# Hidden columns of a SwiGLU feed-forward in tiles of 126 instead of 128

## The chip, the cores and the metric

One core of a Trainium2 chip runs the whole kernel. The metric is the device time of one execution in microseconds, the median over several runs. All arithmetic is in float32; TensorE does it through pairs of rounded parts, as told below.

## The reference

One layer of a flow-matching backbone over 512 latent tokens and 256 context tokens, 2048 features each: a modulated RMSNorm, one input projection shared by gated linear attention and a gated short convolution, one output projection with a gated residual, then a second modulated RMSNorm and a SwiGLU feed-forward with a hidden width of 5632, a gated residual and a last RMSNorm. The part that the change touches:

```python
def swiglu(h, wg, wu, wd):
    return (jax.nn.silu(h @ wg) * (h @ wu)) @ wd

h2 = modulate(rmsnorm(x_next, norm2_g[i]), sh2, sc2)
x_next = x_next + gt2 * swiglu(h2, w_ffn_gate[i], w_ffn_up[i], w_ffn_down[i])
...
return rmsnorm(x, final_g)
```

## The kernel before

Activations lie transposed: features on the 128 partitions, the 512 tokens along the row. Every product is written as three matmuls (`mm3`, L78): both operands are kept as a high part (rounded by a cast on ScalarE) and a low part (the difference, by VectorE), and low x high, high x low and high x high are added up in PSUM. A unit of weights is 128 x 1024 numbers, 512 KB. `load_w` (L106) brings one unit into one of four `raw` buffers by a DMA that SP issues (L103), casts it to `whi` (L87) and subtracts to `wlo` (L88); there are three buffers of each. All matmuls stand at L75.

The feed-forward part begins at L761. The hidden width of 5632 is cut into `HT` = 44 tiles of 128, and the tiles into groups of eight: five groups of eight and one of four. For each hidden tile, `proj_units` multiplies two units of gate weights and two of up weights with the 16 feature tiles of `h2` into the PSUM banks `ag` and `au`, 48 matmuls each. The trace calls a matmul by these names. `swiglu` (L762) makes silu(ag) x au and splits it into the pair `act`. When a group is done, its down pass runs over the 16 output tiles: it loads a unit of `wfd`, multiplies it with the group's `act` pairs into `acc` (24 matmuls for a group of eight) and adds the gated result to the residual `xn` (L793). The last group is done by halves of the tokens, so that the final norm of the first half lies beside the second half's matmuls.

In the first group VectorE also works off the last 16 tiles of the modulation: `mod_some` (L343) loads two half rows of `wm2` per tile through the same `raw` buffers and sums each against `cbc` (L351). It is called after each hidden tile but the first:

```python
            run(proj_units(ag, wfg[ht], h2), proj_units(au, wfu[ht], h2))
            swiglu(ag, au, act[-1], ALL)
            mod_some(2.5, 64)
        if gi == 0:
            mod_finish(48, 64)
```

With 2.5, two and three tiles alternate. The first hidden tile goes by halves of the tokens together with the norm. In this text the hidden tiles of the first group are numbered from 0, and a tile's four units are its two of gate and its two of up weights.

The order on each engine is made by a scheduler when the kernel is built: instructions of one engine may stand in another order than in the code, and each engine then goes through its own list strictly.

Of the kernel before, what the change touches and what calls it, by code (L numbers as in the profile page):

```python
# [28 lines left out]
HT = FFN // P  # L29
# [4 lines left out]
# columns of the "cols" input  # L34
C_G1, C_G2, C_FG, C_BMOD, C_GLA, C_CONV = 0, 16, 32, 48, 144, 146
NCOLS = 170
# square constant blocks of the "cst" input
B_ID, B_TRIF, B_TRIB, B_SUFF, B_SUFB, B_MF, B_MB, B_ONE, B_ONE16, B_SELX, B_SELC = range(11)
NBLK = 11
# columns of the "sm" input  # L40
# [5 lines left out]
def tile_hybrid_block(  # L46
# [30 lines left out]
    def mm3(o, l, r, start, stop):  # L77
        """l, r: (high, low) parts; the three products that float32 can hold."""  # L78
        mm(o, l[1], r[0], start, False)
        mm(o, l[0], r[1], False, False)  # L80
        mm(o, l[0], r[0], False, stop)
# [8 lines left out]
    def split_scaled(hi, lo, src, scale):  # L90
        """Parts of src * scale, with a scale per partition."""
        nc.scalar.activation(hi, src, AF.Copy, scale=scale)
        nc.vector.scalar_tensor_tensor(lo, src, scale, hi.bitcast(F32), op0=ALU.mult, op1=ALU.subtract)  # L93

    def split_shifted(hi, lo, src, shift):
        """Parts of src + shift, with a shift per partition."""
        nc.scalar.activation(hi, src, AF.Identity, bias=shift)
        nc.vector.scalar_tensor_tensor(lo, src, shift, hi.bitcast(F32), op0=ALU.add, op1=ALU.subtract)  # L98
# [7 lines left out]
    def load_w(src, k, eng=None):  # L106
        """One unit of weights, split into its parts, as [128, k, n]."""
        r = load_raw(src)
        n = r.shape[-1]
        hi = wpool.tile([P, 1024], F32R, tag="whi", name="whi", bufs=3)  # L110
        lo = wpool.tile([P, 1024], F32R, tag="wlo", name="wlo", bufs=3)
        split(hi[:, :n], lo[:, :n], r, eng)
        return (hi[:, :n].rearrange("p (k n) -> p k n", k=k),
                lo[:, :n].rearrange("p (k n) -> p k n", k=k))
# [7 lines left out]
    def rsqrt_of_sum(pool, s, scale, n):  # L122
        """1 / sqrt(s * scale + eps): square root and reciprocal, then one Newton step."""
        ms = pool.tile([P, n], F32, tag="rs_m", name="rs_m", bufs=2)
        t = pool.tile([P, n], F32, tag="rs_t", name="rs_t", bufs=2)
        r = pool.tile([P, n], F32, tag="rs_r", name="rs_r", bufs=2)
        nc.vector.tensor_scalar(ms, s, scale, EPS, op0=ALU.mult, op1=ALU.add)
        nc.scalar.activation(t, ms, AF.Sqrt)
        nc.vector.reciprocal(r, t)
        nc.vector.tensor_tensor(t, r, r, op=ALU.mult)  # L130
        nc.vector.tensor_tensor(t, t, ms, op=ALU.mult)
        nc.vector.tensor_scalar(t, t, -0.5, 1.5, op0=ALU.mult, op1=ALU.add)
        nc.vector.tensor_tensor(r, r, t, op=ALU.mult)
        return r

    def row_bcast(ps, pool, r):
        """ps[m, 128 * tt + t] = r[t, tt] for every m."""
        for tt in range(r.shape[-1]):
            dg = pool.tile([P, P], F32, tag="rb_d", name="rb_d", bufs=2)
            nc.vector.tensor_scalar(dg, ident, r[:, tt : tt + 1], None, op0=ALU.mult)  # L140
            mm(tok(ps, tt), ones, dg, tt == 0, True)

# [15 lines left out]
    # ======== K projection behind the stream of the scale columns ========  # L158
    # The rows of x and ctx are scaled by g1 * (1 + scale) only: their norm and the shift's share
    # are applied to the products of this part and the next.  # L160
# [12 lines left out]
    # Silu of the zeros brings in the table before c is there  # L173
# [3 lines left out]
    def mod_cols(src, c0, n):  # L177
        """silu(c) and silu(c_ctx) times n * 128 columns of w_mod: [128 columns, n, (x, ctx)] in PSUM."""
# [92 lines left out]
    # ======== V projection of heads 0 and 1 behind the stream of the shift columns ========  # L271
# [6 lines left out]
    def shift_chunk(i):  # L278
        """Chunk i of hx and hc from the scaled rows: norm, then the shift."""
        for n, h, rb, q in ((SEQ, hx[i], rbx, 0), (CTX, hc[i], rbc, 1)):  # L280
            t = hcpool.tile([P, n], F32, tag=f"sq{q}", name="ht", bufs=2)
            nc.gpsimd.tensor_tensor(t, h[0].bitcast(F32), h[1].bitcast(F32), op=ALU.add)
            nc.vector.tensor_tensor(t, t, rb, op=ALU.mult)
            sh = shs[:, i, q : q + 1]
            if q == 0:
                nc.vector.tensor_scalar(t, t, sh, None, op0=ALU.add)
                split(h[0], h[1], t)
                hraw[i] = t
            else:
                split_shifted(h[0], h[1], t, sh)  # L290
# [10 lines left out]
    def lf_finish(pl, a, n):  # L301
        """Sum of the four partial sums, as rows of lfT."""
# [41 lines left out]
    def mod_some(n, last):  # L344
        """n more of the tiles of 128 features; n may be a fraction."""
# [15 lines left out]
    # ======== V projection of heads 2 and 3; the shift's share of K and of the first V ========  # L361
    def shares(i):
        """Chunk i of the low rank of ctx, and one unit of weights of bias = shift @ w."""
# [65 lines left out]
    def log_gates(pool, tag, pzs, las):  # L429
        """la = log_sigmoid(z) = min(z, 0) - ln(1 + exp(-|z|)); its 1 / 16 is in the constants."""  # L430
# [8 lines left out]
    def proj_units(acc, wsrc, x, units=(0, 1), part=ALL):  # L439
        """acc = (weight columns)^T x, for one tile of 128 columns; yields after each unit of weights."""  # L440
        for n, u in enumerate(units):
            w = load_w(wsrc[u], 8)
            for k in range(8):
                mm3(acc[:, part], sl(w, ALL, k), sl(x[8 * u + k], ALL, part), n == 0 and k == 0, n == 1 and k == 7)
            yield

    def proj_pair(accs, wsrcs, x, units, part, ws=None, eng=None):
        """Two tiles of columns over one part of the tokens, side by side; ws: the first units, if at hand;
        eng: what makes the low parts of the first units, if not VectorE.

        Returns the last units."""
        for n, u in enumerate(units):
# [4 lines left out]
            for k, (acc, w) in ([(k, a) for a in aw for k in range(8)] if kept else  # L457
                                [(k, a) for k in range(8) for a in aw]):
                mm3(acc[:, part], sl(w, ALL, k), sl(x[8 * u + k], ALL, part), n == 0 and k == 0, n == 1 and k == 7)
# [7 lines left out]
    # ======== context states ========  # L467
# [54 lines left out]
    def weave(stages, fill):  # L522
        """A chain's stages between units of the projections, so that TensorE has work while it waits."""
# [9 lines left out]
    # ======== gated linear attention per head, gated short convolution in between ========  # L533
# [17 lines left out]
    def do_gla(h):  # L551
        """One head over blocks of 128 tokens; within a block, decays are relative to its middle."""
# [7 lines left out]
        for d in range(2):  # L560
# [8 lines left out]
            # the column of the middle, whose own decay is one, carries the decay from the block's start to it  # L569
# [26 lines left out]
        # o as [tokens, values], two blocks of tokens to a bank  # L596
# [25 lines left out]
        # per-head norm  # L622
# [8 lines left out]
        # back to [values, tokens]; gain and swish gate  # L631
# [43 lines left out]
    # ======== output projection, gated residual ========  # L675
# [17 lines left out]
    def square(m, t, acc):  # L693
        """Adds t^2 to acc."""
# [5 lines left out]
    def row_scale(sums):  # L700
        """1 / rms of the rows of one half, the same on every partition; sums: tiles of squares to add up."""
# [11 lines left out]
    # the last two tiles go by halves of the tokens, so that the norm of the first half is hidden  # L713
# [47 lines left out]
    # ======== FFN ========  # L761
    def swiglu(ag, au, dst, part):  # L762
        t = big()[:, part]
        nc.scalar.activation(t, ag[:, part], AF.Silu)  # L764
        nc.vector.tensor_tensor(t, t, au[:, part], op=ALU.mult)
        split(dst[0][:, part], dst[1][:, part], t)

    groups = [(8 * g, min(8, HT - 8 * g)) for g in range((HT + 7) // 8)]
    for gi, (h0, nh) in enumerate(groups):
        act = []  # L770
        for ht in range(h0, h0 + nh):
# [11 lines left out]
            mod_some(2.5, 64)  # L783
# [4 lines left out]
        for m in range(KD):  # L788
            acc = abank("acc")
            w = load_w(wfd[m][:, h0 * P : (h0 + nh) * P], nh)  # L790
            for k in range(nh):
                mm3(acc, sl(w, ALL, k), act[k], k == 0, k == nh - 1)
            nc.vector.scalar_tensor_tensor(xn[m], acc, modv[:, 48 + m : 49 + m], xn[m], op0=ALU.mult, op1=ALU.add)  # L793

    # ======== last part of the FFN and final norm, by halves of the tokens ========
    put_t = {}

    def put(i, hf, rb):
        """One half of tile i of the output; two tiles to a store."""
# [10 lines left out]
    # tiles of the last half that get their gain ahead of the norm, for GpSimd to finish  # L810
# [3 lines left out]
    for hf, part in enumerate(parts):  # L814
        for m in range(KD):
# [4 lines left out]
            for k in range(nh):  # L820
                mm3(acc[:, part], [tok(t, k) for t in wl_[m]], sl(act[k], ALL, part), k == 0, k == nh - 1)
# [17 lines left out]
def _constants(np):  # L839
# [6 lines left out]
    # sums from the middle of the block; the column that would be zero sums the first half (forward) or second  # L846
# [19 lines left out]
def _layout(np, inputs):  # L866
    f = lambda n: np.asarray(inputs[n], dtype=np.float32)

    def ktiles(w):
        """[2048, n * 128] -> [n, 2 units, 128, 8 * 128]"""  # L870
        n = w.shape[1] // P
        return w.reshape(2, 8, P, n, P).transpose(3, 0, 2, 1, 4).reshape(n, 2, P, 1024)

    def kpairs(w):
        """[2048, 512] -> [8, 128, 2 * 512]"""
        return w.reshape(8, 2, P, 512).transpose(0, 2, 1, 3).reshape(8, P, 1024)

    def colmaj(v):
# [30 lines left out]
        "wfg": ktiles(f("w_ffn_gate")[0]),  # L909
        "wfu": ktiles(f("w_ffn_up")[0]),  # L910
        "wfd": f("w_ffn_down")[0].reshape(HT, P, KD, P).transpose(2, 1, 0, 3).reshape(KD, P, FFN),
# [20 lines left out]
```

## Time and profile before

| | |
|---|---|
| median of 3 runs | 2478.17 us (2476.71 to 2481.11) |
| span of the profiled execution | 2479.1 us |
| its own time beside the span | not given apart from it |
| TensorE matmuls | 2420.8 us busy, 98%, 11270 instructions |
| VectorE, ScalarE, GpSimd | 42%, 28%, 6% |
| granted TensorE clock | 0.991 on average |
| gate, up and down products | from 1001.9 us (first ag matmul) to the end |

Busy times are shares of the span. A plain float32 matmul counts as two instructions in the trace, so the trace has more matmuls (11270) than the program's order (10503). Matmuls are pipelined: the duration of one, about 389 ns for 512 columns, is longer than the distance between two. For what a matmul costs, read a run of them in the chain of waits and divide by their number.

### The profile page before, as it was taken

What the parts mean: (1) busy time and instruction counts of PE and PEld (TensorE: products, weight loads), DVE (VectorE), ACT (ScalarE), POOL (GpSimd) and SP (SyncE); (2) the same over time, 40 slices, a digit from 0 to 9 for tenths busy, and PEclk for the clock granted to TensorE, in tenths of its full rate; (3) what the DMA queues carried; (4) which work ended last, traced back from release to release, by engine and by line L of the source; (5) the groups of instructions that cost most, each with busy time, mean ns of one, the idle gap of its engine ahead of it and who ended that gap; (6) DMA issues with size and microseconds to landing.
All of it is one profiled execution on the core that took longest, in us unless ns stands there. A gap on an engine that the chain in (4) does not pass through costs nothing.

```text
span 2479.1 us, 27638 instructions
## 1 busy us (share of the span) xinstructions
PE 2420.8 (98%) x11270; PEld 1953.0 (79%) x11270; DVE 1029.9 (42%) x1393; ACT 691.1 (28%) x942; POOL 144.9 (6%) x140
## 2 busy tenths in 40 slices
PE   8999999999999999899999999999999999999997
PEld 5755667787888888788888888888888888888887
DVE  3555155565655533755432233223322232223335
ACT  3522155332323322422212222222122212221232
POOL 2422000000000011300000000000000000000003
PEclk9999999999999999899999999999999999999998
DMA  9763455556553433366433233233322333323231
GB/s 325 231 224 107 161 196 166 177 184 196 187 195 128 161 98 98 112 208 209 125 97 99 94 102 94 95 100 94 101 94 95 101 94 100 96 94 102 94 107 73
DMA packets 117835, 335.45 MB, mean 135 GB/s; under 512 B 12203, under 2 KB 32811, under 8 KB 117580
## 3 DMA queue, kind: packets, MB, share of 16 engines
q1 hardware_dynamic: 117708, 333.69, 41.8%
q8 instruction: 88, 1.44, 0.2%
q14 instruction: 39, 0.32, 0.0%
HBM read 329.44 MB, written 4.19 MB: 135 GB/s over the span
## 4 chain that ended last, share of the span: by engine, by line
PE 78%; DMA 12%; DVE 5%; issue 3%; ACT 2%; SPq 0%; POOL 0%; DVEq 0%; ACTq 0%; POOLq 0%
PE acc L75 41%; PE ag L75 17%; PE au L75 16%; DMA raw<-wm 10%; DVE wlo L88 2%; PE pm L75 1%; DVE raw L351 1%; DMA raw<-wfg 1%; PE pl L75 1%; ACT whi L87 0%; DMA big<-wsh 0%; PE pb L75 0%; DVE mlo L98 0%; PE po L75 0%; DVE big L752 0%
## 5 line engine op out<-in xcount | busy, mean ns | idle before, releaser
L88 DVE TENSOR_TENSOR wlo<-raw,whi 128x1024 fp32r<-128x1024 f32 x386 | 476.3, 1235 | 639.6 <-ACT whi L87 639.4
L87 ACT CAST whi<-raw 128x1024 fp32r<-128x1024 f32 x388 | 407.2, 1051 | 1191.6 <-PE acc L75 558.1
L75 PE MATMUL acc<-big,whi 128*128 128x512 f32 x1280 | 394.0, 389 | 0.0
L75 PE MATMUL ag<-mhi,wlo 128*128 128x512 f32 (+1 forms) x720 | 278.6, 387 | 8.4 <-ACT big L764 6.4
L75 PEld LDWEIGHTS acc<-big,whi 128*128 128x128 f32 x1280 | 240.3, 188 | 49.8
L75 PE MATMUL ag<-mlo,whi 128*128 128x512 f32 (+1 forms) x720 | 277.9, 386 | 0.0
L75 PE MATMUL ag<-mhi,whi 128*128 128x512 f32 (+1 forms) x720 | 277.6, 386 | 0.0
L75 PE MATMUL au<-mhi,wlo 128*128 128x512 f32 (+1 forms) x720 | 277.4, 385 | 0.1
L75 PE MATMUL au<-mlo,whi 128*128 128x512 f32 (+1 forms) x720 | 277.1, 385 | 0.0
L75 PE MATMUL au<-mhi,whi 128*128 128x512 f32 (+1 forms) x720 | 277.0, 385 | 0.0
L75 PE MATMUL acc<-hhi,wlo 128*128 128x512 f32 x640 | 260.7, 408 | 7.0 <-DVE wlo L88 6.2
L75 PE MATMUL acc<-hlo,whi 128*128 128x512 f32 x640 | 252.6, 395 | 0.2 <-DVE hlo L93 0.2
L75 PE MATMUL acc<-hhi,whi 128*128 128x512 f32 x640 | 252.0, 394 | 0.0
L351 DVE CUSTOM_DVE_ANT_0 raw<-raw,cbc 128x1024 f32<-128x1024 f32 x128 | 156.5, 1224 | 228.4 <-DMA raw<-wm 226.1
L75 PE MATMUL acc<-big,wlo 128*128 128x512 f32 x640 | 249.0, 389 | 0.0
L75 PEld LDWEIGHTS ag<-mhi,wlo 128*128 128x128 f32 x720 | 136.5, 190 | 35.7 <-ACT big L764 6.6
L793 DVE SCALAR_TENSOR_TENSOR xn<-acc,modv,xn 128x512 f32<-128x512 f32 x80 | 60.1, 751 | 246.9 <-PE acc L75 246.9
L698 POOL TENSOR_TENSOR sacc<-sacc,sqn 128x256 f32<-128x256 f32 (+1 forms) x41 | 44.2, 1079 | 2017.2 <-ACT sqn L696 2016.8
L75 PEld LDWEIGHTS ag<-mlo,whi 128*128 128x128 f32 x720 | 136.6, 190 | 26.8
L75 PEld LDWEIGHTS au<-mhi,wlo 128*128 128x128 f32 x720 | 135.7, 189 | 27.7 <-DVE wlo L88 1.0
L75 PEld LDWEIGHTS ag<-mhi,whi 128*128 128x128 f32 x720 | 136.4, 189 | 26.7
L75 PEld LDWEIGHTS au<-mlo,whi 128*128 128x128 f32 x720 | 135.7, 188 | 26.8
(202 smaller groups left out, 2768.5 us busy)
## 6 DMA issues: line engine op xcount, KB each, us to landing
raw<-wm SPq DMA_DIRECT2D x128, 512.0 KB, 4.4
raw<-wfg SPq DMA_DIRECT2D x89, 512.0 KB, 3.3
raw<-wfu SPq DMA_DIRECT2D x89, 512.0 KB, 3.3
raw<-wfd SPq DMA_DIRECT2D x80, 512.0 KB, 3.6
raw<-wc SPq DMA_DIRECT2D x48, 512.0 KB, 4.1
raw<-wo SPq DMA_DIRECT2D x34, 512.0 KB, 3.3
big<-wsc SPq DMA_DIRECT2D x64, 256.0 KB, 5.6
big<-wsh SPq DMA_DIRECT2D x64, 256.0 KB, 5.7
```

Of the source, the lines that this page charges most:

```text
L75: nc.tensor.matmul(o, l, r, start=start, stop=stop, skip_group_check=True)
L87: nc.scalar.copy(hi, src)
L88: (eng or nc.vector).tensor_tensor(lo, src, hi, op=ALU.subtract)
L351: nc.vector.tensor_tensor_reduce(out=w, in0=w, in1=cbc[:, hf * 1024 : hf * 1024 + 1024], scale=1.0, scalar=0.0, op0=ALU.mult, op1=ALU.add, ...
L698: nc.gpsimd.tensor_tensor(acc, acc, s, op=ALU.add)
L793: nc.vector.scalar_tensor_tensor(xn[m], acc, modv[:, 48 + m : 49 + m], xn[m], op0=ALU.mult, op1=ALU.add)
```

## The change

The columns of the gate and up weights (and the rows of the down weights) are cut into 45 tiles of 126 instead of 44 tiles of 128. 45 x 126 = 5670, so the last tile ends in 38 columns of zeros. The host lays the weights out so: a unit of gate or up weights is 128 x 1008, and the down weights keep rows of 128 per tile of which the last two are zero. The groups become five of seven, one of six and one of four; a unit of a down pass has 896 or 768 columns. `mod_some` gets 3 tiles per hidden tile instead of 2.5, for six calls in the first group instead of seven. Gate and up matmuls write 126 partitions of PSUM, down matmuls contract over 126. Comments were dropped, which shifts line numbers by one to four.

```diff
-HT = FFN // P
+TH = 126
+HT = -(-FFN // TH)
...
-                mm3(acc[:, part], sl(w, ALL, k), sl(x[8 * u + k], ALL, part), n == 0 and k == 0, n == 1 and k == 7)
+                mm3(acc[: w[0].shape[-1], part], sl(w, ALL, k), sl(x[8 * u + k], ALL, part),
+                    n == 0 and k == 0, n == 1 and k == 7)
...
     def swiglu(ag, au, dst, part):
-        t = big()[:, part]
-        nc.scalar.activation(t, ag[:, part], AF.Silu)
-        nc.vector.tensor_tensor(t, t, au[:, part], op=ALU.mult)
-        split(dst[0][:, part], dst[1][:, part], t)
-
-    groups = [(8 * g, min(8, HT - 8 * g)) for g in range((HT + 7) // 8)]
+        t = big()[:TH, part]
+        nc.scalar.activation(t, ag[:TH, part], AF.Silu)
+        nc.vector.tensor_tensor(t, t, au[:TH, part], op=ALU.mult)
+        split(dst[0][:TH, part], dst[1][:TH, part], t)
+
+    sizes = [7] * 5 + [6, 4]
+    groups = [(sum(sizes[:g]), n) for g, n in enumerate(sizes)]
...
-            mod_some(2.5, 64)
+            mod_some(3, 64)
...
-                mm3(acc, sl(w, ALL, k), act[k], k == 0, k == nh - 1)
+                mm3(acc, sl(w, slice(0, TH), k), sl(act[k], slice(0, TH)), k == 0, k == nh - 1)
...
-                mm3(acc[:, part], [tok(t, k) for t in wl_[m]], sl(act[k], ALL, part), k == 0, k == nh - 1)
+                mm3(acc[:, part], [tok(t, k)[:TH] for t in wl_[m]], sl(act[k], slice(0, TH), part), k == 0, k == nh - 1)
...
+    def htiles(w):
+        w = np.concatenate([w, np.zeros((D, HT * TH - FFN), np.float32)], axis=1)
+        return w.reshape(2, 8, P, HT, TH).transpose(3, 0, 2, 1, 4).reshape(HT, 2, P, 8 * TH)
+
+    def hrows(w):
+        t = np.zeros((HT, P, D), np.float32)
+        t[:, :TH] = np.concatenate([w, np.zeros((HT * TH - FFN, D), np.float32)]).reshape(HT, TH, D)
+        return t.reshape(HT, P, KD, P).transpose(2, 1, 0, 3).reshape(KD, P, HT * P)
...
-        "wfg": ktiles(f("w_ffn_gate")[0]),
-        "wfu": ktiles(f("w_ffn_up")[0]),
-        "wfd": f("w_ffn_down")[0].reshape(HT, P, KD, P).transpose(2, 1, 0, 3).reshape(KD, P, FFN),
+        "wfg": htiles(f("w_ffn_gate")[0]),
+        "wfu": htiles(f("w_ffn_up")[0]),
+        "wfd": hrows(f("w_ffn_down")[0]),
```

On all engines the order is the same up to the feed-forward part. Inside the first group it moves at two places. The first is SP's list of loads between hidden tiles 1 and 2 (raw is the buffer; wfg, wfu and wm2 are gate weights, up weights and modulation rows). Before:

```order
L103 DMA raw_7572<-wfu 128x1024
L103 DMA raw_7607<-wm2 128x1024
L103 DMA raw_7610<-wm2 128x1024
L103 DMA raw_7613<-wm2 128x1024
L103 DMA raw_7616<-wm2 128x1024
L103 DMA raw_7623<-wfg 128x1024
L103 DMA raw_7653<-wfg 128x1024
```

The same place after the change:

```order
L104 DMA raw_7572<-wfu 128x1008
L104 DMA raw_7607<-wm2 128x1024
L104 DMA raw_7610<-wm2 128x1024
L104 DMA raw_7613<-wm2 128x1024
L104 DMA raw_7616<-wm2 128x1024
L104 DMA raw_7619<-wm2 128x1024
L104 DMA raw_7622<-wm2 128x1024
L104 DMA raw_7629<-wfg 128x1008
L104 DMA raw_7659<-wfg 128x1008
```

Six half rows of modulation now stand ahead of tile 2's weights instead of four; the same holds in each of tiles 1 to 5, where four and six alternated.

The second place is VectorE's list at tile 2 (wlo is a weight split, ISA with cbc the sum of a modulation row, the row behind it reads out its result). Before:

```order
L88 TENSOR_TENSOR wlo_7626<-raw_7623,whi_7625 128x1024
L351 ISA raw_7748,modacc_73<-raw_7748,cbc_76 128x1024
L351 ISA modacc_73 128x1
L88 TENSOR_TENSOR wlo_7656<-raw_7653,whi_7655 128x1024
L351 ISA raw_7751,modacc_73<-raw_7751,cbc_76 128x1024
L351 ISA modacc_73 128x1
L765 TENSOR_TENSOR big_7602<-big_7602,au_7479 128x512
L88 TENSOR_TENSOR wlo_7686<-raw_7683,whi_7685 128x1024
```

After:

```order
L89 TENSOR_TENSOR wlo_7632<-raw_7629,whi_7631 128x1008
L89 TENSOR_TENSOR wlo_7662<-raw_7659,whi_7661 128x1008
L352 ISA raw_7754,modacc_73<-raw_7754,cbc_76 128x1024
L352 ISA modacc_73 128x1
L768 TENSOR_TENSOR big_7602<-big_7602,au_7479 126x512
L352 ISA raw_7757,modacc_73<-raw_7757,cbc_76 128x1024
L352 ISA modacc_73 128x1
L89 TENSOR_TENSOR big_7481<-big_7602,big_7480 126x512
L89 TENSOR_TENSOR wlo_7692<-raw_7689,whi_7691 128x1008
```

Both weight splits of the gate now come ahead of the first modulation row of tile 2, where a row stood between them. From tile 3 on, the list of a tile with six half rows reads as it did before.

More of the change, by code (lines that the diff above doesn't have):

```diff
@@ L458, in proj_pair @@
                                 [(k, a) for k in range(8) for a in aw]):
-                mm3(acc[:, part], sl(w, ALL, k), sl(x[8 * u + k], ALL, part), n == 0 and k == 0, n == 1 and k == 7)
+                mm3(acc[: w[0].shape[-1], part], sl(w, ALL, k), sl(x[8 * u + k], ALL, part),
+                    n == 0 and k == 0, n == 1 and k == 7)
         return ws
```

## The prediction

> **What bounds the kernel now.** I read the page's busy shares first, then the stretches of the feed-forward part, then the chain of waits inside it.
>
> ```profile
> span 2479.1 us, 27638 instructions
> PE 2420.8 (98%) x11270; PEld 1953.0 (79%) x11270; DVE 1029.9 (42%) x1393; ACT 691.1 (28%) x942; POOL 144.9 (6%) x140
> PEclk9999999999999999899999999999999999999998
> ```
>
> TensorE is busy for 98% of the span at an almost full granted clock, so its instructions are what the time is made of, wherever nothing holds them up. A table of three stretches shows the feed-forward part: the first group's gate and up products, the first down pass, and the second group's gate and up products (columns: length, then busy time of each engine with its count, granted clock, DMA share, GB/s).
>
> ```profile
> 1046.00:1194.01 148.01, 147.91 (x651) 121.77 (x650) 76.33 (x103) 35.53 (x40) 0.00 (x0) 1.00 0.65 212
> 1194.01:1281.05 87.04, 87.04 (x385) 72.10 (x385) 32.15 (x33) 17.41 (x17) 0.00 (x0) 1.00 0.32 97
> 1281.05:1455.13 174.08, 174.08 (x769) 144.19 (x769) 48.97 (x47) 41.20 (x47) 0.00 (x0) 1.00 0.31 97
> ```
>
> In the last two, TensorE never pauses, the clock is 1.00, and VectorE, ScalarE and the DMA engines are busy for well under half. In the first one the DMA share doubles to 0.65 and VectorE works half the time, because the last 16 tiles of modulation rows are loaded there too. So there are two regimes: a matmul costs its pitch everywhere, and in the first group the weights may come too late.
>
> The pitch comes from the chain of waits, which holds whole runs of matmuls:
>
> ```profile
> 1194.01 87.04 PE acc L75 x384
> 1281.05 10.88 PE ag L75 x48
> 1291.93 10.88 PE au L75 x48
> 2415.83 20.07 PE acc L75 x164
> 2444.88 17.05 PE acc L75 x142
> ```
>
> 10.88 / 48 and 87.04 / 384 both give 226.67 ns for a matmul of 512 moving columns. The last row has matmuls of 256 columns: 17.05 / 142 = 120.1 ns. Halving the columns takes off 106.6 ns, so 512 columns stream in 213.2 ns and 13.5 ns of each matmul do not depend on the moving columns. The row before it, 20.07 / 164 = 122.4, is the same form with a few stops.
>
> **More matmuls: +32.6 us.** A matmul of this kind moves 512 token columns past a stationary tile. The change makes the stationary tile two columns narrower for gate and up (126 instead of 128) and takes two rows less of contraction in the down product. Neither is the moving dimension. Gate and up grow from 44 to 45 tiles, each 2 x 16 x 3 = 96 matmuls: +96. The down product is 16 output tiles x 3 matmuls per hidden tile: +48. Together +144, which the order of instructions confirms (10,503 matmuls become 10,647). All of them stand on TensorE's own path: 144 x 226.67 ns = 32.64 us. The last group keeps four tiles, so its halved matmuls do not grow in number.
>
> Does a partly filled array change the pitch? The trace has rows with a partly filled array: 33 rows (pzs), and 32 columns (pb).
>
> ```profile
> L75 PEld LDWEIGHTS acc<-big,whi 128*128 128x128 f32 x1280 | 240.3, 188 | 49.8
> L75 PEld LDWEIGHTS pzs<-gatet,lfT x24: 182/186/187, 319.9 to 379.6; 33*128 33x128 f32 x24
> L75 PE MATMUL pzs<-gatet,lfT x24: 589/589/693, 319.9 to 380.0; 33*128 33x512 f32 x24
> L75 PE MATMUL pz<-big,cstt x12: 590/592/593, 332.8 to 343.0; 128*128 128x512 f32 x12
> L75 PEld LDWEIGHTS pz<-big,cstt x12: 188/188/190, 332.5 to 342.6; 128*128 128x128 f32 x12
> L75 PEld LDWEIGHTS pb<-raw,silsh x64: 106/109/110, 256.2 to 314.0; 128*32 128x32 f32 x64
> L75 PE MATMUL pb<-raw,silsh x64: 592/592/617, 256.2 to 314.4; 128*32 128x512 f32 x64
> ```
>
> Filled (pz), 33 rows (pzs) or 32 columns (pb), the matmul's median is 589 to 592 ns. Only the weight load follows the columns: 109 ns for 32, 188 for 128, that is 0.82 ns per column. Two columns less save 1.6 ns of a load that already runs beside the matmul (188 is below the pitch of 226.67). I take a change of the pitch of nothing. For the ends I use the part of the pitch that is not streaming, 13.5 ns: it can go at most altogether, and per column (2 / 128 of it) it moves by 0.2 ns, which over the 6,768 matmuls touched (45 x 96 + 96 more for the first tile's halves, 41 x 48, and 384 halves at the end) is 1.4 us. So the term is 31 to 34 us, short of the rivals below.
>
> The Trainium skill has a rule that speaks against the change. "TensorE: Matmul & The Clock Gate", section "Weight-path perf modes — Fast Weight Load (FWL) and DoubleRow", says that a fast weight load is on when the number of weights is 128 and the type is not FP32; with 126 the gate and up loads would lose it. The trace does not bear out that it is on now: the load of the feed-forward matmuls (188 ns, in the rounded float32 type) is as long as that of the plain float32 matmuls of pz (188). What it would cost is a rival below.
>
> **The first group: +3 us.** VectorE and SP set the pace of loading here, and this is where the change moves instructions. First the chain of waits through the first group. The wlo rows are the low-part splits of the first unit of tiles 2 to 7, except the last, which belongs to the third unit of tile 7.
>
> ```profile
> 1040.95 10.92 PE ag L75 x48
> ...
> 1053.46 1.24 DVE wlo L88
> ...
> 1077.99 1.24 DVE wlo L88
> ...
> 1099.45 1.24 DVE wlo L88
> ...
> 1122.78 1.24 DVE wlo L88
> ...
> 1143.24 1.24 DVE wlo L88
> ...
> 1168.15 1.24 DVE wlo L88
> ...
> 1181.60 1.15 DVE wlo L88
> 1182.79 11.22 PE au L75 x48
> ```
>
> Tile 1 starts at 1040.95, and a tile takes 2 x 10.88 = 21.76, so TensorE wants tile k at 1040.95 + 21.76 (k - 1). The steps between the splits are 24.53, 21.46, 23.33, 20.46, 24.91. By SP's order these steps hold ten, eight, ten, eight, ten loads (four of weights, and six or four of modulation rows): 24.26 on average with ten, 20.96 with eight, 1.65 for each load more. The stream is slower than TensorE's 21.76 whenever three tiles of modulation stand between. At tile 2 it is 8 us ahead, at tile 7 the lead is used up: TensorE starts the down pass at 1194.01 instead of 1040.95 + 7 x 21.76 = 1193.27, 0.74 late. Why a step of ten loads takes so long, VectorE's timeline of tile 2 shows (start, length, what; in brackets the wait and what ended it):
>
> ```profile
> 1053.46 1.23 DVE L88 TENSOR_TENSOR wlo<-raw,whi 128x1024 fp32r<-128x1024 f32 x1 [1.04 <-ACT whi L87]
> 1059.71 1.23 DVE L351 CUSTOM_DVE_ANT_0 raw<-raw,cbc 128x1024 f32<-128x1024 f32 x1 [5.02 <-DMA raw<-wm]
> 1060.86 0.09 DVE L351 DVE_READ_ACCUMULATOR2_ANT modacc<- 128x1 f32 x1
> 1060.86 1.22 DVE L88 TENSOR_TENSOR wlo<-raw,whi 128x1024 fp32r<-128x1024 f32 x1
> 1065.37 1.23 DVE L351 CUSTOM_DVE_ANT_0 raw<-raw,cbc 128x1024 f32<-128x1024 f32 x1 [3.29 <-DMA raw<-wm]
> ...
> 1070.47 1.23 DVE L351 CUSTOM_DVE_ANT_0 raw<-raw,cbc 128x1024 f32<-128x1024 f32 x1 [0.38 <-DMA raw<-wm]
> ...
> 1074.83 1.22 DVE L88 TENSOR_TENSOR wlo<-raw,whi 128x1024 fp32r<-128x1024 f32 x1
> ...
> 1077.99 1.22 DVE L88 TENSOR_TENSOR wlo<-raw,whi 128x1024 fp32r<-128x1024 f32 x1 [0.80 <-ACT whi L87]
> ```
>
> There are four raw buffers. Each use on VectorE frees one, and SP then issues the fourth load ahead. VectorE's order asks for a modulation row right behind a weight split, so it waits out a whole transfer: split, wait, row, wait, row and so on, four transfers in a row per step, some 4.5 us each (1060.94 to 1065.37 for the second).
>
> Now the change. With 3 instead of 2.5 tiles of modulation per hidden tile over six tiles, every tile from 1 to 5 has ten loads, and tile 6 has two rows. Tile 1 gets two loads more: the split of tile 2 moves from 1053.46 to 1053.46 + 2 x 1.65 = 1056.8. In tile 2 the new order puts two weight splits ahead of the first row, so only three transfers stand in a row: 24.26 - 4.4 = 19.9, and tile 3 is at 1076.7. Tiles 3 to 5 have the order of the present steps of ten: 1076.7 + 3 x 24.26 = 1149.5 for tile 6. The last unit of tile 5 is split 21.4 after its first (as 1074.83 - 1053.46), at 1125.2 + 21.4, and is ready 1.2 later at 1147.8; TensorE wants it at 1040.95 + 4 x 21.76 + 16.32 = 1144.3. It waits 3.5 us. Tile 6 then keeps up: its third unit, 13.4 after the first as in tile 7 now, is ready at 1164.1, and the delayed TensorE comes to it at 1149.75 + 10.88 + 3.5 = 1164.1. So 3.5 late instead of 0.74: about +3. The ends: no wait at all, -0.7; or tile 2 gains nothing from its order and the steps are the longest seen (24.91): tile 5's last unit at 1056.8 + 3 x 24.91 + 21.4 + 1.2 = 1154.1, 9.8 late, +9. Behind VectorE's waiting rows stand the splits of the next units, so a late row is at once a late weight.
>
> **Edits that I cost at nothing.** A seventh group adds a down pass boundary. At a boundary TensorE must not reach the last hidden tile before its product is split:
>
> ```profile
> L765 DVE TENSOR_TENSOR big<-big,au 128x512 f32<-128x512 f32 x43 | 29.5, 686 | 112.6 <-PE au L75 112.6
> L88 DVE TENSOR_TENSOR big<-big 128x512 fp32r<-128x512 f32 x43 | 29.4, 684 | 0.1
> L87 ACT CAST big<-big 128x512 fp32r<-128x512 f32 x43 | 26.6, 618 | 36.6 <-DVE big L765 36.6
> ```
>
> That is 686 + 618 + 684, with one weight split of about 1221 between them: 3.2 us. The matmuls of the other tiles cover it: 7 x 3 x 226.67 ns = 4.8 us now, 4.1 with seven tiles, 3.4 with six. With hand-overs the group of six may lose up to 0.5 us once. The 16 more down tiles bring 16 more splits and additions on VectorE and casts on ScalarE, in passes where these are busy for 32 and 17 of 87 us. Weight units of 1008, 896 and 768 columns are shorter than 1024; where four buffers have slack, as in all later groups, nothing is won or lost by that. Code ahead of the feed-forward part stands in the same order as before.
>
> **The sum.** 32.6 + 3 = 35.6. Against the profiled execution's span, 2479.1 + 35.6 = 2514.7. The page gives no time around the span; the median of the three runs, 2478.17, is 0.9 below it, which puts the median after at 2513.8.
>
> **Rivals.**
> - Starving: the loads of the first group cost TensorE 5 to 9 us instead of 3, because the narrower rows (4032 bytes a partition) land later or tile 2's order gains nothing. The DMA share of 0.65 speaks for it, the walk through the order against it. 2478.2 + 32.6 + 5 to 9 gives 2516 to 2520, a little more if all go wrong. Chance 0.18.
> - Faster: the 13.5 ns beyond streaming are spent on bringing a full array's weights in, and fall away when it is not full. Place: every gate, up and down matmul, 6,768 of them. Altogether that is worth 91 us, 2423 in the end; it decides from 35.6 / 6768 = 5.3 ns on. The filled and unfilled rows above, alike within 3 ns of 590, speak against it. Chance 0.04.
> - Fast loads lost: the gate and up loads get longer. If the column part of a load, 128 x 0.82 = 105 ns, is a halved one and doubles, a load takes 293 ns, above the pitch by 66; 45 x 96 = 4320 of them cost 286 us, about 2800. The equal 188 ns of the two types speaks against it. Chance 0.03. This is the rule of the Trainium skill named above.
> - Nothing: the added work is hidden. With TensorE at 174.08 of 174.08 us there is no place for it. Chance 0.01, 2478.
>
> **How the numbers follow.** My forecast, 2509 to 2516 with 2513.8 as its centre, has 0.72; the starving case 0.18; 0.02 stays for something unnamed above 2522. The range 2508 to 2522 holds the first two. About 0.2% (5 us) is what a measurement of this kernel can tell from no change: faster 0.04, same 0.01, slower 0.95.
>
> **What would show it.** Right: runs of ag and au of 48 matmuls still 10.88 us long, passes of 336 and 288 acc matmuls of 76.16 and 65.28, a load of 126 columns 1 to 2 ns below 188, 144 more matmuls, and between the start of tile 1 and the first down pass 6 x 21.76 = 130.6 plus 3 to 4 us, the wait at the low part of tile 5's last unit. Wrong: a pitch other than 226.67 in the ag and au runs but not in wout's, waits on raw<-wfg in later groups, or a first group that ends without a wait or more than 9 us late.

## The result, and the profile after

The changed kernel takes 2538.9 us (median of 3 runs, 2537.84 to 2538.94) against 2478.17 (2476.71 to 2481.11). The recorded ratio is 1.0238, its 95% interval 1.0221 to 1.0254. The medians differ by 60.7 us, where 35.6 were forecast. The sign was right, the time lies 17 us above the end of the range.

First the page of the changed kernel, the rows that answer to those of before:

```profile
span 2536.0 us, 28071 instructions
PE 2475.0 (98%) x11414; PEld 1974.6 (78%) x11414; DVE 1049.5 (41%) x1431; ACT 698.4 (28%) x964; POOL 145.0 (6%) x140
PEclk9999999999999999999999999999999999999999
```

11414 - 11270 = 144 more matmuls, as counted. TensorE is still busy for 98% at an almost full granted clock, so the time that was not forecast lies in busy TensorE, not in gaps. The table of stretches for the gate and up products of the second group, and for the first down pass (length, busy time of each engine with its count, granted clock, DMA share, GB/s):

```profile
1253.51:1408.99 155.48, 155.48 (x673) 125.03 (x673) 42.10 (x41) 35.33 (x41) 0.00 (x0) 1.00 0.30 92
1177.32:1253.51 76.19, 76.19 (x338) 63.09 (x337) 30.27 (x33) 15.87 (x17) 0.00 (x0) 1.00 0.34 100
```

Seven tiles are 14 runs of 48 matmuls: 155.48 / 14 = 11.11 us each, not 10.88. TensorE never pauses there, the clock is 1.00, the other engines and the DMA are no busier than before. The down pass of 336 takes 76.19, which is 226.76 ns a matmul, against 226.67 before. So the matmuls with a stationary slice of 126 columns became slower, those that contract over 126 rows did not. The chain of waits shows the same, and the end of the first group (wlo is the split of tile 5's last unit):

```profile
1147.87 1.13 DVE wlo L89
1149.04 5.84 PE au L76 x24
1154.88 11.13 PE ag L76 x48
1166.02 11.30 PE au L76 x48
1177.32 76.19 PE acc L76 x336
1253.51 11.12 PE ag L76 x48
1264.62 11.11 PE au L76 x48
1275.73 11.11 PE ag L76 x48
```

The mean distance between the starts of two gate or up matmuls, over the runs of 48 without a stop, is 231.4 ns in the trace (226.67 before), and it is not even: averaged place by place over the runs of the later groups, the 48 distances lie between 225.9 and 235.8 ns, where before each of them was 226.6 to 226.8. TensorE's timeline shows how matmuls and weight loads (PEld) alternate:

```profile
1281.12 0.40 PE L76 MATMUL ag<-mhi,wlo 128*126 128x512 f32 x1
1281.12 0.19 PEld L76 LDWEIGHTS ag<-mlo,whi 128*126 128x126 f32 x1
1281.36 0.40 PE L76 MATMUL ag<-mlo,whi 128*126 128x512 f32 x1
1281.36 0.19 PEld L76 LDWEIGHTS ag<-mhi,whi 128*126 128x126 f32 x1
1281.59 0.39 PE L76 MATMUL ag<-mhi,whi 128*126 128x512 f32 x1
```

The weight load did not get longer. Groups by form in the gate and up products of the second group, before and after in turn (mean ns after the comma):

```profile
L75 PEld LDWEIGHTS au<-mhi,whi 128*128 128x128 f32 x128 | 24.0, 188 | 5.0
L76 PEld LDWEIGHTS au<-mhi,whi 128*126 128x126 f32 x112 | 20.8, 186 | 5.0
L75 PE MATMUL ag<-mhi,whi 128*128 128x512 f32 x128 | 49.8, 389 | 0.0
L76 PE MATMUL ag<-mhi,whi 128*126 128x512 f32 x112 | 44.1, 394 | 0.0
```

The load's mean fell from 188 to 186 ns, as the prediction expected of two columns less. The matmul's record grew from 389 to 394, the same 5 ns as the distance. The starts and ends of the loads in the two traces say where the time goes (medians over the gate and up products of the later groups): a load starts 3 ns behind a matmul's start in both, but the next matmul starts 35 ns behind the load's end before the change and 42 ns behind it after. The time is lost between the end of a load and the start of the matmul behind it.

Where the span's 56.9 us come from, by the traces of the two profiled executions (2479.1 to 2536.0):

| part | us |
|---|---|
| 144 more matmuls at 226.67 ns | +32.6 |
| 4224 gate and up matmuls of tiles 1 to 44 (44 x 96), each 155.48 / 672 = 231.37 instead of 226.67 ns | +19.9 |
| first group: TensorE is 4.3 us behind its own pace at the first down pass (12 runs of 11.11 us after 1039.56 end at 1172.8, the pass starts at 1177.2), 0.74 before | +3.6 |
| from the start of the last group's halved down pass to the end | +1.8 |
| everything ahead of tile 1 | -1.2 |
| left over | +0.2 |

The last two named parts look like differences between executions: the closing stretch, 68.5 us here at a granted clock of 0.88, takes 66.1 to 67.0 us at 0.90 to 0.91 in the traces of three other kernels with the same 45 tiles below, and 66.7 at 0.90 before. The medians differ by 3.8 more than the profiled executions. The execution after took 1.8 us more than its span (2537.84 against 2536.0); with the same 1.8 the profiled one before was near the highest of its three, while the one after was the lowest of its three.

### The profile page after: what moved, and what is told of

Its sections match the earlier page's. It is cut to its first block, busy times and chain, and to the rows that moved or that the text cites. A ratio compares the mean times of both kernels' runs of the same rounds, so it can differ in the third digit from the quotient of the medians.

```text
span 2536.0 us, 28071 instructions
## 1 busy us (share of the span) xinstructions
PE 2475.0 (98%) x11414; PEld 1974.6 (78%) x11414; DVE 1049.5 (41%) x1431; ACT 698.4 (28%) x964; POOL 145.0 (6%) x140
## 4 chain that ended last, share of the span: by engine, by line
PE 79%; DMA 11%; DVE 5%; issue 3%; ACT 1%; SPq 0%; POOL 0%; DVEq 0%; ACTq 0%; POOLq 0%
PE acc L76 40%; PE ag L76 17%; PE au L76 17%; DMA raw<-wm 9%; DVE wlo L89 1%; PE pm L76 1%; DVE raw L352 1%; PE pl L76 1%; DMA raw<-wfg 1%; PE po L76 1%; DMA big<-wsh 0%; DVE mlo L99 0%; PE pb L76 0%; ACT whi L88 0%; PE pd L76 0%
## 5 line engine op out<-in xcount | busy, mean ns | idle before, releaser
L89 DVE TENSOR_TENSOR wlo<-raw,whi 128x1008 fp32r<-128x1008 f32 (+3 forms) x406 | 483.1, 1191 | 671.2 <-ACT whi L88 669.5
L88 ACT CAST whi<-raw 128x1008 fp32r<-128x1008 f32 (+3 forms) x408 | 413.3, 1014 | 1234.3 <-PE acc L76 555.3
L76 PE MATMUL acc<-big,whi 126*128 126x512 f32 x1312 | 404.1, 389 | 0.0
L76 PE MATMUL ag<-mhi,wlo 128*126 128x512 f32 (+1 forms) x736 | 287.8, 391 | 8.3 <-ACT big L767 6.4
L76 PE MATMUL au<-mhi,wlo 128*126 128x512 f32 (+1 forms) x736 | 287.2, 390 | 3.1 <-DVE wlo L89 3.0
L76 PE MATMUL ag<-mhi,whi 128*126 128x512 f32 (+1 forms) x736 | 287.7, 391 | 0.0
L76 PE MATMUL ag<-mlo,whi 128*126 128x512 f32 (+1 forms) x736 | 287.7, 391 | 0.0
L76 PE MATMUL au<-mlo,whi 128*126 128x512 f32 (+1 forms) x736 | 287.1, 390 | 0.0
L76 PE MATMUL au<-mhi,whi 128*126 128x512 f32 (+1 forms) x736 | 287.1, 390 | 0.0
L76 PE MATMUL acc<-big,wlo 126*128 126x512 f32 x656 | 255.2, 389 | 0.0
```

The costliest lines, as they stand in the source:

```text
L76: nc.tensor.matmul(o, l, r, start=start, stop=stop, skip_group_check=True)
L88: nc.scalar.copy(hi, src)
L89: (eng or nc.vector).tensor_tensor(lo, src, hi, op=ALU.subtract)
```

## The experiments

**Number of columns or place of the slice.** The change does two things to a gate or up slice: it has 126 columns, and its slices lie 504 bytes apart instead of 512, so that seven of eight start off the old grid of 512 bytes. The first theory was that the place costs, the second that the number of columns does. Three kernels separate the two. The first is the changed kernel with a unit laid out in steps of 128, of which 126 are loaded:

```diff
-        return (hi[:, :n].rearrange("p (k n) -> p k n", k=k),
+        return (hi[:, :n].rearrange("p (k n) -> p k n", k=k)[:, :, :cols],   # cols = 126, and lo so too
...
+        t = np.zeros((HT, 2, P, 8, P), np.float32)                           # host: 8 x 128 a unit
+        t[..., :TH] = w.reshape(2, 8, P, HT, TH).transpose(3, 0, 2, 1, 4)
```

> The changed kernel, but a unit of gate or up weights keeps a stride of 128 columns in the buffer (two columns of zeros behind each slice of 126, 1024 in all); 45 tiles of 126 columns as before. In the changed kernel the ag and au runs of 48 matmuls take 11.11 us instead of 10.88. Theory A (place of the slice): the slices start every 504 bytes, and loads from such places cost it. Then the runs go back to 10.88 and the time falls by 4.7 ns x 4224 = 20 us to about 2519. Theory B (columns): 126 active columns cost it. Then the runs stay at 11.11 and the time at 2539.

The second is the kernel before (44 tiles) with the same `[:, :, :126]`, and the third the kernel before with full slices of 128 that start every 126 columns:

> The kernel before with 44 tiles and a stride of 128, but only 126 of the 128 columns of each gate and up slice are used, and 126 rows in the down product: 2 of 128 hidden columns are left out. Theory A: runs of 10.88 us, time 2478 as before. Theory B: runs of 11.11 us, 4.7 ns x 4128 = 19 us more, 2497.

```diff
+            return ([hi[:, i * st : i * st + P] for i in range(k)], ...       # st = 126, and lo so too
```

> The kernel before with full slices of 128 columns, but the slices of tiles 1 to 43 start every 126 columns (504 bytes) in the buffer, so neighbours share two columns: other weights are multiplied than the reference's; everything else is as before. Theory A: runs of about 11.1 us, some 19 us more, 2497. Theory B: runs of 10.88, 2478.

Measured: 2543.21 us, ratio 1.0253 (1.0234 to 1.0273; the ratios of this section are to the kernel before as it ran beside each experiment, with medians of 2480.09 to 2481.75 us); 2504.52, ratio 1.0101 (1.0079 to 1.0123); 2493.67, ratio 1.0057 (1.0038 to 1.0076). The chain of waits gives one run of each, in this order:

```profile
1263.64 11.20 PE au L76 x48
```
```profile
1282.31 11.20 PE ag L76 x48
```
```profile
1334.12 11.08 PE au L76 x48
```

With 126 columns in the old places the pitch is 11.20 / 48 = 233.33 ns, worse than in the changed kernel; with all 128 columns at the new places it is 230.8. Each of the two costs by itself, the two costs do not add up (231.4 with both), and both theories in their pure form fall. The second kernel's down passes, over 126 rows, stay at 226.7 a matmul.

**The stall of the first group.** The changed kernel with fewer modulation rows per tile:

```diff
-            mod_some(3, 64)
+            mod_some(8 / 3 + 1e-9, 64)
```

> The changed kernel with 2.67 tiles of modulation per hidden tile in the first group (2 3 3 2 3 3) instead of 3 3 3 3 3 1. In the changed kernel TensorE comes to the first down pass 4.3 us later than 12 runs of 11.11 us after tile 1's start. If the density of modulation loads sets that, it falls to 1 to 2 us and the time by 2 to 3 us to about 2536. If narrower rows or the split order set it, nothing changes: 4.3 us late, 2539.

Measured: 2530.32, ratio 1.0202 (1.0184 to 1.022). Its chain of waits at the end of the first group:

```profile
1151.37 11.11 PE ag L76 x48
1162.48 11.34 PE au L76 x48
1173.82 76.19 PE acc L76 x336
```

From the start of tile 1 to the first pass it takes 133.53 us, 0.25 more than 12 runs, where the changed kernel has 4.3. The number of modulation rows per tile sets that stall, and not the narrower weight rows, which are the same in both; the pitch is unmoved by it (11.11 us a run). The median fell by 8.6 us, more than the 2 to 3 expected; by the traces 4.1 us are the stall and 2.4 the closing stretch (66.1 against 68.5).

The other side of it, the kernel before with 44 tiles of 128 but groups of seven and 3 tiles of modulation:

```diff
-    groups = [(8 * g, min(8, HT - 8 * g)) for g in range((HT + 7) // 8)]
+    sizes = [7] * 5 + [5, 4]
+    groups = [(sum(sizes[:g]), n) for g, n in enumerate(sizes)]
...
-            mod_some(2.5, 64)
+            mod_some(3, 64)
```

> The kernel before, 44 tiles of 128, but in groups of 7 7 7 7 7 5 4 and with 3 tiles of modulation per hidden tile: the grouping of the change alone. Matmuls and their pitch stay (10.88 us for 48, no matmul more). By the prediction's walk through the first group TensorE starts the first down pass 3.5 us late by its own pace, against 0.7 before: about +3 us, 2481. If the wait of the changed kernel (4.3 us) comes from the narrower rows of 4032 bytes, it is gone here: 0.7 late, 2478. A down pass boundary that costs would show beside it as a gap at the later groups.

Measured: 2488.35 (ten runs, 2481.98 to 2493.38), ratio 1.0032 (1.002 to 1.0044). The chain of waits of its profiled execution, the shortest of the ten:

```profile
1144.13 1.15 DVE wlo L88
1145.32 5.74 PE au L75 x24
1151.06 10.88 PE ag L75 x48
1161.94 10.88 PE au L75 x48
1172.82 76.16 PE acc L75 x336
1248.98 10.88 PE ag L75 x48
```

The pitch is the old one, the wait stands at the same split of tile 5's last unit, and the first group ends 4.7 us late (135.28 against 12 x 10.88), 4.0 more than before. From there to the last group's halved pass it takes 1240.32 = 37 x 21.76 + 5 x 76.16 + 54.4 = 1240.3: a seventh group cost nothing at its boundaries in this execution. By the medians the grouping alone costs 8.3 us, where 3 were expected; the trace accounts for 4.0 of them, and as the other nine executions have no trace, the rest stays open.

**A rule for the number of columns?** The kernel before with 124, 120, 112, 96 and 64 of the 128 columns of each tile, at the old 512 bytes (the diff is that of 126, with the number changed):

> The kernel before with 124 of the 128 columns of each gate and up slice used (stride 128; 4 of 128 hidden columns left out). With 126 columns the ag and au runs of 48 took 11.20 us, 233.3 ns a matmul, exactly 16 cycles of a 2.4 GHz clock over 226.7 (with 128). Theory C (reads of four columns, 16 bytes): 124 is a multiple of 4, so the pitch is back at 226.7 or a cycle below. Theory D (any slice that is not full pays): 233.3 stays. Theory E (the pitch has a part that shrinks with the columns read): below 226.7.

> The same with 120 columns (8 of 128 left out), a multiple of 8 (32 bytes). Theory C: 226.7 or a little below, as with 124. If reads go by 32 bytes, 120 is back at 226.7 and 124 is not. Theory D: 233.3.

> The same with 112 columns (16 of 128 left out), a multiple of 16 (64 bytes). Theory C: 226.7 or a little below. If reads go by 64 bytes, 112 is back at 226.7 and 124 and 120 are not. Theory D: 233.3. Theory E: clearly below 226.7, by some 4 cycles (1.7 ns).

> The same with 96 columns (32 of 128 left out), three of the four blocks of 32 columns. If the array's blocks of 32 set it, 96 is back at 226.7 or lower and 126, 124, 120 and 112 all stay at 233.3. Theory D: 233.3. Theory E: about 8 cycles (3.3 ns) below 226.7.

> The kernel before with 64 of the 128 hidden columns of each tile (at the old stride of 512 bytes; the other 64 are left out of gate, up and down products). A slice is then 256 bytes, the unit that the shift runs speak for. If a slice has to be whole pieces of 256 bytes, the gate and up pitch is 226.67 ns and the time 2470 to 2484 us; if only the full 128 columns give that pitch, it is 228 to 234 ns, as with 96 to 126 columns, and the time 2484 to 2507.

**And for the stride?** The kernel before with full slices that start every 124, 120 and 112 columns (496, 480 and 448 bytes):

> The kernel before with full slices of 128 columns that start every 124 columns (496 bytes, a multiple of 16) in the buffer for tiles 1 to 43; neighbours share columns, so other weights are multiplied. Every 504 bytes gave a pitch of 230.8 ns instead of 226.7. If the start has to be a multiple of 16 bytes, 226.7; if of 32 or 64 bytes, between 228 and 233.

> The same, starting every 120 columns (480 bytes, a multiple of 32). 226.7 if 16 or 32 bytes are enough; between 228 and 233 if it takes 64.

> The same, starting every 112 columns (448 bytes, a multiple of 64). 226.7 if a multiple of 64 bytes is enough. If it stays at 228 or more, only the stride of 512 bytes of the kernel before is free of it, or the place is not what counts.

**A constant shift.** Full slices, 512 bytes apart, all but the last of a unit starting 2, 16, 64 or 32 columns later (tiles 1 to 43):

```diff
+            return ([hi[:, j : j + P] for j in [i * P + st * (i < 7) for i in range(k)]], ...   # st = 2, 16, 64 or 32
```

> Full slices of 128 columns in 44 tiles, 512 bytes apart as before, but in tiles 1 to 43 the slices 0 to 6 of every unit start 8 bytes later than before (slice 7 stays; the product is one of other weights). If what costs is a start that is no multiple of 512 bytes, the slices 0 to 6 run above 226.67 ns, by 4 ns as where the slices lay 504 bytes apart (230.83), slice 7 may stay, and the time is about 2480 + 3612 x 4.2 ns = 2495 us. If what costs is that the start moves against 512 bytes from slice to slice, only the two steps around slice 7 can show it: a run of 48 within 0.1 us of 10.88, the time 2477 to 2482.

> The same with 64 bytes (16 columns) instead of 8. Start modulo 512: 228 to 233 ns a matmul, 2485 to 2504 us, and a difference to the run with 8 bytes says that the place counts finely. Change from slice to slice: 226.67 and 2477 to 2482 again.

> The same with 256 bytes (64 columns). Start modulo 512: slow as the two others. If only the start modulo 256 counts: 226.67, 2477 to 2482, while the two others are slow. Change from slice to slice: 226.67 in all three.

> The shift runs once more, with 128 bytes (32 columns): full slices, 512 bytes apart, in tiles 1 to 43 the slices 0 to 6 start 128 bytes later. 8 bytes gave 230.7 ns, 64 bytes 233.1, 256 bytes 226.67. If the start has to be a multiple of 128 bytes, 226.67 ns and 2477 to 2484 us; if of 256, 229 to 234 ns and 2488 to 2505 us.

All of them in one table. The pitch is the mean distance of matmul starts in the trace over the runs of 48 gate and up matmuls without a stop; "start" is how many bytes past a multiple of 256, counted from the tile's start, the slices begin.

| kernel | columns | stride, bytes | start past 256 | pitch, ns | time, us |
|---|---|---|---|---|---|
| before | 128 | 512 | 0 | 226.67 | 2478.17 |
| shift of 256 bytes | 128 | 512 | 0 | 226.67 | 2482.14 |
| shift of 128 bytes | 128 | 512 | 128 | 232.8, later 231.7 | 2507.07 |
| shift of 64 bytes | 128 | 512 | 64 | 233.1 | 2503.16 |
| shift of 8 bytes | 128 | 512 | 8 | 230.7 | 2494.36 |
| stride 126 columns | 128 | 504 | changing | 230.8 | 2493.67 |
| stride 124 columns | 128 | 496 | changing | 232.7 | 2507.15 |
| stride 120 columns | 128 | 480 | changing | 232.2 | 2503.89 |
| stride 112 columns | 128 | 448 | changing | 231.4 | 2501.18 |
| after | 126 | 504 | changing | 231.4 | 2538.90 |
| after, stride 512 | 126 | 512 | 0 | 233.3 | 2543.21 |
| before, 126 columns | 126 | 512 | 0 | 233.3 | 2504.52 |
| before, 124 | 124 | 512 | 0 | 226.7, later 228.3 | 2484.67 |
| before, 120 | 120 | 512 | 0 | 233.3 | 2505.46 |
| before, 112 | 112 | 512 | 0 | 229.0, later 233.3 | 2505.31 |
| before, 96 | 96 | 512 | 0 | 230.0 | 2493.70 |
| before, 64 | 64 | 512 | 0 | 230.0 | 2530.73 |

Times of a single execution stand in most rows (the kernel before took 2475.76 to 2481.75 beside them); the pitch, from some 4000 distances of one trace, is what tells them apart. One run of each of the four shifts from the chain of waits, 256, 128, 64 and 8 bytes:

```profile
1336.52 10.88 PE au L76 x48
```
```profile
1334.29 11.12 PE ag L76 x48
```
```profile
1336.93 11.19 PE au L76 x48
```
```profile
1291.33 11.07 PE au L76 x48
```

A shift that is the same for neighbouring slices costs as much as a changing one, unless it is 256 bytes. So it is the place of the start that counts, modulo 256 bytes among the shifts tried, and not its change from slice to slice. With 64 columns a slice is exactly 256 bytes and starts in its place, and its pitch is 230.0: a whole piece of 256 bytes does not help, the columns missing from 128 cost as such. No count below 128 kept the old pitch throughout, and there is no order in the counts: 124 comes nearest to it, 126, 120 and for the most part 112 have 233.3, 96 and 64 have 230.0. The loads of 96 and 64 columns take 161 and 134 ns, less than the 188 of a full one, and the pitch is higher all the same, so the length of the load is not what binds. The groups by form for 96 and for 64 columns:

```profile
L76 PEld LDWEIGHTS au<-mhi,whi 128*96 128x96 f32 x556 | 89.7, 161 | 38.2
```
```profile
L76 PEld LDWEIGHTS au<-mhi,whi 128*64 128x64 f32 x552 | 74.2, 134 | 51.6
```

With 64 columns the next matmul starts 93 ns behind a load's end (median): the shorter load ends sooner and wins nothing. The number of columns loaded is in each of these kernels also the number of PSUM partitions that the matmul writes, so they cannot tell a partial load from a partial write.

The time with 64 columns, 2530.73 where at most 2507 was expected, is not the pitch alone. A table of stretches shows why (the clock stands ahead of the last two numbers):

```profile
1281.30:1455.13 173.83, 173.83 (x757) 101.67 (x756) 47.64 (x46) 40.38 (x47) 0.00 (x0) 1.00 0.30 97
2428.00:2513.00 85.00, 84.17 (x399) 82.73 (x398) 30.28 (x65) 20.74 (x45) 20.86 (x28) 0.53 0.11 39
```

In the last 101 us the granted clock falls to about half, and this closing stretch takes 34 us longer than before, where it was 66.7 us at 0.90. Why stays open.

**The full load back in the changed kernel.** A test of the sum: everything of the change stays, but a gate or up slice is laid out and loaded as 128 columns, with two columns of zeros:

```diff
-        return w.reshape(2, 8, P, HT, TH).transpose(3, 0, 2, 1, 4).reshape(HT, 2, P, 8 * TH)
+        t = np.zeros((HT, 2, P, 8, P), np.float32)
+        t[..., :TH] = w.reshape(2, 8, P, HT, TH).transpose(3, 0, 2, 1, 4)
+        return t.reshape(HT, 2, P, 8 * P)
```

> The changed kernel in everything (45 tiles of 126, groups of seven, 3 tiles of modulation) but that a gate or up slice is laid out and loaded as 128 columns, the last two of them zeros, so that the load is a full one at a stride of 512 bytes. If the missing 20 us are the pitch of loads that are not full or not in their place, runs of 48 are back at 10.88 us and 144 matmuls, a stall of 4 us and a tail of 2 are left: 2538.9 - 4224 x 4.7 ns = 2519 us, ratio 1.014 to 1.018. If the pitch has another cause that belongs to the 45 tiles (shorter transfers, other buffers, the PSUM rows that the product of two reads), it stays at 231 to 233 ns and the time at 2536 to 2543 us.

Measured: 2520.93 (2519.47 to 2525.17), ratio 1.0162 (1.0145 to 1.0179). Its span, and its chain of waits from the end of the first group:

```profile
span 2519.9 us, 28106 instructions
```
```profile
1149.57 1.15 DVE wlo L89
1150.77 7.35 PE au L76 x24
1158.12 10.88 PE ag L76 x48
1168.99 10.88 PE au L76 x48
1179.88 76.19 PE acc L76 x336
1256.06 10.91 PE ag L76 x48
1266.97 10.88 PE au L76 x48
```

The old pitch is back with 45 tiles and 144 more matmuls. By the traces its span is 40.8 us above that of before: 32.6 for the matmuls, 8.1 for the first group (139.37 against 12 x 10.88 = 130.56 is 8.8 late, 0.74 before), 0.1 for the rest. Against the changed kernel it wins 16.1 us of span: about 20 by the pitch, 1.6 at the end, less 4.5 in the first group and 0.8 ahead of it. It is the fastest of the forms with 45 tiles that were run, and still slower than the kernel before. Full slices together with fewer modulation rows per tile were not run.

## Why the prediction was wrong, point by point

- **More matmuls, +32.6: right.** 144 more in the trace; with the pitch restored they are the greatest part of the 40.8 us.
- **"I take a change of the pitch of nothing": this step failed.** The pitch of the gate and up matmuls rose from 226.67 to 231.4 ns, which is worth 19.9 of the 25 us that were missed. The prediction's first sign of being wrong came true: the output projection's matmuls stayed at 226.75 ns. The error was in the evidence. The rows of pz, pzs and pb give durations, of plain float32 matmuls; what was needed were distances, of matmuls in the rounded type with a narrower load between them. The trace of before had none of these with fewer than 128 columns. The upper end was mis-sized too: the 13.5 ns of the pitch that do not stream were allowed to go altogether but to grow by 0.2 only. They grew by 4.7, and by 6.7, half of themselves, in three of the kernels. With the same measure upwards, 13.5 ns for each of 4320 matmuls, the term's end would have been 58 us higher, and the result inside.
- **"Fast loads lost": wrong mechanism, right direction.** The loads did not grow to 293 ns, they fell from 188 to 186, and 2520 to 2543 us is far from 2800. The Trainium skill ("TensorE: Matmul & The Clock Gate", "Weight-path perf modes — Fast Weight Load (FWL) and DoubleRow") makes 128 weights a condition of its fast loads. The runs agree in this much, that no number below 128 kept 226.67 ns throughout. But full loads of 128 that start off the 256 bytes are slowed as well, and with fewer columns no load was longer, so the runs do not show that this rule is the cause.
- **The faster rival** fell: in no run here was the pitch below 226.67 ns with less than a full slice.
- **The first group, +3: the place right, the size by luck.** The last and longest wait stands where the walk put it, at the low part of tile 5's last unit, ready at 1149.0 instead of 1147.8. But it is 1.6 us of 3.0, and three shorter waits for weight splits, from tile 3 on, stand ahead of it, which the walk did not have. The list of waits up to the first down pass (us in total, times, longest):

```profile
PE au L76 <- DVE wlo L89: 3.0, 4, 1.6
```

  The splits ahead of it, predicted at 1056.8, 1076.7, 1101 and 1125, stand in the chain of waits of the changed kernel at

```profile
1057.97 1.22 DVE wlo L89
...
1077.82 1.22 DVE wlo L89
...
1103.12 1.22 DVE wlo L89
...
1125.91 1.22 DVE wlo L89
```

  although tile 1 began 1.2 to 1.4 us earlier than the walk assumed: against that start the loads came 2 to 3.5 us later than priced. The slower pitch hid this, since TensorE itself asked for the weights later. At the old pitch the same step cost 4.0 and 8.1 us more than before in two traces (groups of seven; full loads): within the ends given, above the value taken, and no run shows why the two differ.
- **Boundaries and shorter units at nothing: right.** Between the first down pass and 2440 us, TensorE waited for nothing that the list of waits shows, and the kernel with groups of seven and full slices adds up without a rest.
- **The span against the median.** The prediction took the median to lie 0.9 below the profiled execution's span. The run after shows 1.8 us beside the span; if the profiled execution before had as much, it was a long one, about 2.7 us above its median. Of the 25 us missed, 3.8 are such differences between medians and profiled executions.

Settled: 20 of the 25 us beyond the forecast are the pitch of the gate and up matmuls; either of the two things that the change does to a slice raises it, and a full load in its old place brings it back. Not settled: why. The pitch repeats after 24 matmuls (8 slices by 3 products) in the changed kernel and lies between 225 and 236 ns there; the loss stands between a load's end and the next matmul's start, but no run shows what the matmul waits for there.

## What to carry to other kernels

A stationary slice that is not full, or does not start in its place, can cost 2 to 3% of every matmul (4.7 to 6.7 of 226.67 ns here) although its load is hidden and no longer: in this kernel it paid to pad a slice of 126 with zeros to 128 columns and to keep its start on 256 bytes. Price a change of the operand by the distance between starts in a run of that type, not by the duration of a record, and let an unknown price grow as far as it is allowed to shrink. A stall behind a loader depends on the consumer's pace; when that changes too, the two terms are not to be added up separately.

## What was not expected of the hardware

- 128 columns on a multiple of 256 bytes: 226.67 ns, that is, at the prediction's 0.4164 ns a column, the time of 544 columns. Else up to 233.33, the time of 560; in three kernels exactly that.
- The same instructions run at two paces in one execution: 112 columns at 229.0 ns in the first group and 233.3 in all later ones, 124 columns at 226.7 and then 228.3, the shift of 128 bytes at 232.8 and then 231.7.
- Rows cost nothing here: contraction over 126, 96 or 64 of 128 rows leaves the down pass at 226.7 to 227.0 ns.
- With half of the hidden columns left out, the granted clock was 0.53 over 85 us at the end of the run; before, it was 0.92 over the last 85 us.
